# Weight parts of an FFN that begin 16-byte pieces apart inside larger buffers

## The chip, the core and the metric

The kernel runs on one core of one Trainium2 chip. The core has five engines that work side by side, each through its own queue of instructions: TensorE (PE, matrix products; its weight loads are shown apart as PEld), VectorE (DVE), ScalarE (ACT), GpSimd (POOL) and SyncE (SP, which issues the DMA transfers here). They meet in a memory of 128 rows (partitions), called SBUF; results of products land in a second one, PSUM. The metric is the device time of one execution in microseconds. Before the change it is 877.67 us, the median of three runs that lie between 876.88 and 879.24.

## The reference

One decoder layer in float32 with 512 tokens and 1024 channels. A first sub-layer has two token mixers (a sparse attention in three branches, and a gated delta rule), gates, an output projection and a layer norm. The change lies in the second sub-layer, a gated MLP with a short convolution:

```
def conv_ffn(x, w_up, conv_w, w_down):          # w_up 1024 x 5632, w_down 2816 x 1024
    h = causal_dwconv(x @ w_up, conv_w)         # width 3, along the tokens
    gate, val = jnp.split(h, 2, axis=-1)
    return (jax.nn.silu(gate) * val) @ w_down

x = layer_norm(DEEPNORM_ALPHA * x + f, ln2_g, ln2_b)   # f = conv_ffn(x, ...)
```

## The kernel before

Every large product is made of three. A float32 matrix is split in two parts, `hi`, its copy in the shortened format that TensorE takes at full pace (`F32R`), and `lo`, the rest. With both sides split, hi x hi, hi x lo and lo x hi are summed in PSUM. So each weight tile costs a copy on ACT (`wh`, line 215) and a subtraction, in the FFN on DVE (`wl`, line 219), before TensorE can use it.

`split_w` does this for one unit of weights. A unit is 512 KB: 128 partitions with 1024 values (4096 bytes) each. SP loads it into one of three `raw` buffers (line 208). Then its two halves of 512 values follow one another: the copy into one of three `wh` buffers, the subtraction into one of three `wl` buffers. Each of these holds 2048 bytes a partition, exactly one half. A buffer is written again when TensorE has done its last product with the half that it held. The buffers lie in the pool `stream`, which is used through the whole kernel, and begin at addresses that are multiples of 256 bytes; so do all the other large tiles.

The FFN runs in this order.

- **Output projection and first layer norm** (lines 953 to 975). For each of four row tiles of 128 tokens, TensorE makes two products of 512 columns (`pw`) from the parts `woh` and `wol` of the projection's weights. DVE adds the residual (line 971), takes the statistics (972) and does the norm (927 to 934, with one step on POOL, line 247). Eight transposes (line 946) turn the row tile, and ACT and DVE split it into `mh` and `ml` (948, 949). The transposes of a row tile stand in TensorE's queue inside the next tile's products; those of the last one stand behind the first two units of the FFN. This hides the norm.
- **First two channel tiles** (p = 0 and 1, lines 978 to 998). Their four units are split whole (lines 987 and 988) into buffers of their own, and their products run in two halves of 256 columns each.
- **Up projection** (lines 1006 to 1027). For each of the 20 other channel tiles, and for gate and value (b = 0, 1), one unit goes through `split_w`, and `product` (lines 229, 231, 232) makes 24 products of 512 columns into `pu`. The weight parts are the stationary side here: 128 columns of 512 bytes are loaded for each product, while `mh` or `ml` moves through. Behind them ACT, DVE and POOL do the convolution, the gate and the split into `ah` and `al`.
- **Down projection** (lines 1041 to 1066). For each half of the 1024 output channels, 11 units of two k tiles are split, and `down` (lines 1034 to 1036) makes 24 products a unit into four PSUM tiles `pdn`. The weight parts are the moving side here: rows of 512 values, 2048 bytes, stream through, and `ah` or `al` is loaded. In the second half the last four units go through other buffers (`th`, `tl`, lines 1045 to 1051), so 11 + 7 units use `split_w`. The residual and the last layer norm follow.

A planner sets each engine's order from the program's order and the times at which it believes buffers to be free; the waits come from the reads and writes of each tile's bytes.

Of the kernel before, what the change touches and what calls it, by code (L numbers as in the profile page):

```python
# [11 lines left out]
F32R = mybir.dt.float32r  # L12
# [5 lines left out]
S = 512  # L18
D = 1024
KD = 8  # L20
# [47 lines left out]
def layout(a):  # L68
# [18 lines left out]
    for i in range(8):  # L87
# [38 lines left out]
BUFS = {"in": 3, "st": 6, "mid": 4, "out": 3, "att": 4, "ob": 1, "qf": 2, "kq": 2, "lx": 1, "pg": 2, "pd": 2, "pa": 3,  # L126
        "raw": 3, "wh": 3, "wl": 3, "q2": 4, "mg": 6, "mr": 4}
# [3 lines left out]
def body(ctx: ExitStack, tc: tile.TileContext, d, out):  # L131
    nc = tc.nc
    V, A, G, PE = nc.vector, nc.scalar, nc.gpsimd, nc.tensor
# [42 lines left out]
    wp = ctx.enter_context(tc.tile_pool(name="stream", bufs=2))  # L176
# [25 lines left out]
        A.activation(xh[:, k, :], xr, AF.Copy)  # L202
        V.tensor_tensor(xl[:, k, :], xr, xh[:, k, :].bitcast(F32), op=OP.subtract)

    def split_w(src, shape, eng, first=A):

        raw = wp.tile(shape, F32, name="raw", bufs=BUFS["raw"])
        nc.sync.dma_start(out=raw, in_=src)
        half = shape[1] // 2
        hi, lo = [], []  # L210
        for i in range(2):
            r = raw[:, i * half:(i + 1) * half]
            wh = wp.tile([128, half] + list(shape[2:]), F32R, name="wh", bufs=BUFS["wh"])
            if first is A:
                A.activation(wh, r, AF.Copy)  # L215
            else:
                first.tensor_copy(wh, r)
            wl = wp.tile([128, half] + list(shape[2:]), F32R, name="wl", bufs=BUFS["wl"])
            eng.tensor_tensor(wl, r, wh.bitcast(F32), op=OP.subtract)  # L219
            hi += [wh[:, k] for k in range(half)]  # L220
            lo += [wl[:, k] for k in range(half)]
        return hi, lo

    def product(ps, w, m, n):

        (wh, wl), (mh_, ml_) = w, m
        first = None
        for k in range(n):
            i = PE.matmul(ps, wh[k], mh_(k), start=(k == 0), stop=False)  # L229
            first = first or i  # L230
            PE.matmul(ps, wh[k], ml_(k), start=False, stop=False)  # L231
            PE.matmul(ps, wl[k], mh_(k), start=False, stop=(k == n - 1))  # L232
        return first
# [3 lines left out]
    def gemm_t(u, eng=None, after=None):  # L237
        w = split_w(d["wT"][u], [128, KD, 128], E("ws", u, "G"), E("wh", u, "A"))
        ps = gps()
        first = product(ps, w, (lambda k: xh[:, k, :], lambda k: xl[:, k, :]), KD)  # L240
        if after is not None:
            tc.add_manual_dep(first.ins, after.ins.name, mybir.DependencyInfo(
                mybir.DependencyClass.NoSync, mybir.DependencyReason.SCHED_ONLY), reason="its rows have no room before")
        return ps
# [601 lines left out]
    at = 0  # L846
# [33 lines left out]
    for i in range(8):  # L880
        src = (oT + yT)[i]
# [4 lines left out]
    for m in range(8):  # L886
        while done < min(16, max(2 * m + 4, BUFS["mg"] + 2)):
            merge(done, mg2)
            done += 1
        wh, wl = split_w(d["wm"][m], [128, KD, 128], V)  # L890
        t = []
        for b in range(2):
            ps = pm.tile([128, S], F32, name=f"pm{b}")
            product(ps, (wh[4 * b:], wl[4 * b:]), (lambda k: yoh[:, 4 * b + k, :], lambda k: yol[4 * b + k]), 4)
            v = MG.pop(2 * m + b)
            V.scalar_tensor_tensor(v, v, 1.0, ps, op0=OP.add, op1=OP.mult)
            t.append(v)
        V.tensor_tensor(t[0], t[0], t[1], op=OP.add)
        A.activation(mh[:, m, :], t[0], AF.Copy)
        V.tensor_tensor(ml[:, m, :], t[0], mh[:, m, :].bitcast(F32), op=OP.subtract)  # L900
        raw = wp.tile([128, D], F32, name="raw", bufs=BUFS["raw"])
        nc.sync.dma_start(out=raw, in_=d["wo"][m])
        A.activation(woh[:, m, :], raw, AF.Copy)
        V.tensor_tensor(wol[:, m, :], raw, woh[:, m, :].bitcast(F32), op=OP.subtract)
# [19 lines left out]
    def layer_norm(r, gb, st, after=lambda i: None):  # L924

        mv = ln.tile([128, 2], F32, name="mv", bufs=2)
        V.bn_aggr(out=mv, in_=st)
        rs = ln.tile([128, 1], F32, name="rs", bufs=2)
        V.tensor_scalar(rs, mv[:, 1:2], LN_EPS, None, op0=OP.add)  # L929
        rsqrt(rs, rs, 1)  # L930
        for i in range(2):
            cs = slice(i * 512, (i + 1) * 512)
            V.scalar_tensor_tensor(r[:, cs], r[:, cs], mv[:, 0:1], gb[:, 0, cs], op0=OP.subtract, op1=OP.mult)
            V.scalar_tensor_tensor(r[:, cs], r[:, cs], rs, gb[:, 1, cs], op0=OP.mult, op1=OP.add)
            after(i)
# [44 lines left out]
    first = {}  # L980
    for p in range(NE):
        for b in range(2):
            raw = wp.tile([128, KD, 128], F32, name="raw", bufs=BUFS["raw"])
            nc.sync.dma_start(out=raw, in_=d["up"][p, :, b])
            wh = fw.tile([128, KD, 128], F32R, name=f"wh{p}{b}")
            wl = fw.tile([128, KD, 128], F32R, name=f"wl{p}{b}")
# [15 lines left out]
    ah = fp.tile([128, NF, S], F32R, name="ah")  # L1002
    al = fp.tile([128, NF, S], F32R, name="al")
    pdn = psum("pdn", 1)
    for p in range(NF):
        g = []
        for b in range(2):
            if p < NE:
                ps = first[p, b][2]
            else:  # L1010
                wu = split_w(d["up"][p, :, b], [128, KD, 128], V)
                ps = pu.tile([128, S], F32, name=f"pu{b}")
                product(ps, wu, (lambda k: mh[:, k, :], lambda k: ml[:, k, :]), KD)
            w = fcw[:, b * NF + p, :]
            acc = fs.tile([128, S], F32, name=f"fa{b}", bufs=2)
            A.activation(acc, ps, AF.Copy, scale=w[:, 2:3])  # L1016
            for i in (1, 0):
                n = 2 - i
                V.scalar_tensor_tensor(acc[:, n:], ps[:, :S - n], w[:, i:i + 1], acc[:, n:],  # L1019
                                       op0=OP.mult, op1=OP.add)  # L1020
            g.append(acc)
        th = fs.tile([128, S], F32, name="fth", bufs=1)
        A.activation(th, g[0], AF.Tanh, scale=0.5)
        V.scalar_tensor_tensor(th, th, 1.0, g[0], op0=OP.add, op1=OP.mult)
        G.tensor_tensor(th, th, g[1], op=OP.mult)  # L1025
        A.activation(ah[:, p, :], th, AF.Copy)
        V.tensor_tensor(al[:, p, :], th, ah[:, p, :].bitcast(F32), op=OP.subtract)
# [4 lines left out]
    def down(ps, k, t, wh, wl):  # L1032
        ts = slice(t * 128, (t + 1) * 128)
        PE.matmul(ps, ah[:, k, ts], wh, start=(k == 0), stop=False)  # L1034
        PE.matmul(ps, ah[:, k, ts], wl, start=False, stop=False)  # L1035
        PE.matmul(ps, al[:, k, ts], wh, start=False, stop=(k == NF - 1))  # L1036

    stats = []
    for i in range(2):
        cs = slice(i * 512, (i + 1) * 512)  # L1040
        pss = [pdn.tile([128, S], F32, name=f"pdn{t}") for t in range(TT)]
        last = []
        for k0 in range(0, NF, 2):
            if i == 1 and k0 >= NF - NL:
                raw = wp.tile([128, 2, S], F32, name="raw", bufs=BUFS["raw"])
                nc.sync.dma_start(out=raw, in_=d["down"][i, k0 // 2])
                hi = tw.tile([128, 2, S], F32R, name=f"th{k0}")
                lo = tw.tile([128, 2, S], F32R, name=f"tl{k0}")
                A.activation(hi, raw, AF.Copy)
                V.tensor_tensor(lo, raw, hi.bitcast(F32), op=OP.subtract)  # L1050
                last += [(k0 + kk, hi[:, kk], lo[:, kk]) for kk in range(2)]
                continue
            hi, lo = split_w(d["down"][i, k0 // 2], [128, 2, S], V)
            for kk in range(2):
                for t in range(TT):
                    down(pss[t], k0 + kk, t, hi[kk], lo[kk])
        for t in range(TT):
            for k, hi, lo in last:
                down(pss[t], k, t, hi, lo)
            r = x1[:, t, :]  # L1060
            V.scalar_tensor_tensor(r[:, cs], r[:, cs], ALPHA, pss[t], op0=OP.mult, op1=OP.add)
            if i == 0:
                stats.append(ln.tile([128, 2, 6], F32, name=f"st{t}"))
            V.bn_stats(out=stats[t][:, i, :], in_=r[:, cs])
            if i == 1:
                ts = slice(t * 128, (t + 1) * 128)
                layer_norm(r, ln2, stats[t], lambda j: nc.sync.dma_start(
                    out=out[ts, j * 512:(j + 1) * 512], in_=r[:, j * 512:(j + 1) * 512]))
# [22 lines left out]
```

## Time and profile before

| what | us |
|---|---|
| median of three runs | 877.67 (876.88 to 879.24) |
| the profiled execution | 879.48 |
| its span, first to last instruction | 877.7 |
| TensorE busy in the span | 847.1 (97%) |
| DVE, ACT, POOL busy | 562.6, 384.8, 159.9 |
| up projection's 960 products behind the first two channel tiles | 217.6 |

How to read it: times in a profile are counted from the start of the span. An instruction's busy time on TensorE is modelled and overlaps that of the next one, so the pace of products is read from their starts. "Idle before" is the time for which an engine stood still ahead of a group, with the instruction that ended it. The granted clock is the share of TensorE's full clock that it was given, 0.988 in the mean over the span.

### The profile page before, as it was taken

How to read it: one execution, taken by the hardware profiler on the slowest of the kernel's cores; microseconds unless marked ns; L12 is line 12 of the kernel's file. 1: busy time of each engine (PE TensorE's matmuls, PEld its weight loads, DVE VectorE, ACT ScalarE, POOL GpSimd, SP SyncE). 2: the span in 40 equal slices, each digit the busy share in tenths (PEclk: the TensorE clock that was granted, in tenths of full speed). 3: DMA queues.
4: the chain of work that ended last, by engine and by line, in shares of the span. 5: the costliest groups of instructions: out<-in, count | busy, mean ns of one | idle time of the engine just before them, and what ended most of it. 6: DMA issues, size and time to landing. Idle time of an engine off the chain costs nothing.

```text
span 877.7 us, 11725 instructions
## 1 busy us (share of the span) xinstructions
PE 847.1 (97%) x4292; PEld 698.2 (80%) x4292; DVE 562.6 (64%) x1159; ACT 384.8 (44%) x855; POOL 159.9 (18%) x141
## 2 busy tenths in 40 slices
PE   9899799999999999999999999999999999999996
PEld 8677678777777678888888898888888888888885
DVE  4755759995766987485457636777766677423337
ACT  5463268567446767443234104444444444322220
POOL 1232342324424320112100001111111111000001
PEclk9999799999999999999999999999999999999999
DMA  7323110101111001254356001333333323333322
GB/s 244 119 72 96 48 50 25 49 25 49 48 50 48 25 26 49 73 159 137 135 192 240 24 1 49 96 96 97 96 97 98 97 98 98 106 100 99 96 73 96
DMA packets 22954, 76.33 MB, mean 87 GB/s; under 512 B 3184, under 2 KB 3568, under 8 KB 22640
## 3 DMA queue, kind: packets, MB, share of 16 engines
q1 hardware_dynamic: 22896, 75.57, 26.9%
q8 instruction: 34, 0.56, 0.2%
q14 instruction: 24, 0.20, 0.1%
HBM read 73.47 MB, written 2.10 MB: 86 GB/s over the span
## 4 chain that ended last, share of the span: by engine, by line
PE 86%; DVE 9%; ACT 2%; issue 1%; DMA 1%; POOL 0%; SPq 0%; DVEq 0%; ACTq 0%; POOLq 0%
PE pu L229 9%; PE pu L231 9%; PE pu L232 9%; PE gps L229 7%; PE gps L232 7%; PE gps L231 7%; PE pdn L1036 5%; PE pdn L1034 5%; PE pdn L1035 5%; PE pout L805 2%; DVE tmp L495 2%; PE pw L969 2%; PE pw L970 2%; PE pm L232 2%; PE pm L231 2%; PE pw L968 2%
## 5 line engine op out<-in xcount | busy, mean ns | idle before, releaser
L215 ACT ACTIVATE wh<-raw 128x512 fp32r<-128x512 f32 (+1 forms) x198 | 122.6, 622 | 224.4 <-PE pu L231 99.3
L219 DVE TENSOR_TENSOR wl<-raw,wh 128x512 fp32r<-128x512 f32 (+1 forms) x172 | 134.5, 784 | 133.4 <-ACT wh L215 130.5
L229 PE MATMUL pu<-mh,wh 128*128 128x512 f32 (+1 forms) x384 | 142.7, 372 | 0.0
L231 PE MATMUL pu<-ml,wh 128*128 128x512 f32 (+1 forms) x384 | 142.6, 371 | 0.0
L232 PE MATMUL pu<-mh,wl 128*128 128x512 f32 (+1 forms) x384 | 142.6, 371 | 0.0
L229 PE MATMUL gps<-xh,wh 128*128 128x512 f32 x320 | 131.3, 411 | 0.8 <-DVE acc L372 0.5
L232 PE MATMUL gps<-xh,wl 128*128 128x512 f32 x320 | 130.4, 407 | 0.0
L231 PE MATMUL gps<-xl,wh 128*128 128x512 f32 x320 | 129.0, 403 | 0.0
L219 POOL TENSOR_TENSOR wl<-raw,wh 128x512 fp32r<-128x512 f32 x48 | 63.5, 1324 | 170.5 <-ACT wh L215 101.0
L232 PEld LDWEIGHTS pu<-mh,wl 128*128 128x128 f32 x384 | 72.3, 188 | 12.6
L229 PEld LDWEIGHTS pu<-mh,wh 128*128 128x128 f32 x384 | 72.3, 188 | 12.6
L231 PEld LDWEIGHTS pu<-ml,wh 128*128 128x128 f32 x384 | 72.3, 188 | 12.3
L1019 DVE SCALAR_TENSOR_TENSOR fa<-pu,fcw,fa 128x511 f32<-128x511 f32 x88 | 65.7, 746 | 10.7 <-ACT fa L1016 9.2
L229 PEld LDWEIGHTS gps<-xh,wh 128*128 128x128 f32 x320 | 61.3, 191 | 12.9 <-issue 1.3
L232 PEld LDWEIGHTS gps<-xh,wl 128*128 128x128 f32 x320 | 61.0, 191 | 11.2 <-POOL wl L219 0.5
L231 PEld LDWEIGHTS gps<-xl,wh 128*128 128x128 f32 x320 | 61.1, 191 | 10.6 <-issue 0.4
L1025 POOL TENSOR_TENSOR fth<-fth,fa 128x512 f32<-128x512 f32 x22 | 28.7, 1302 | 214.0 <-DVE fa L1019 214.0
L1035 PE MATMUL pdn<-wl,ah 128*128 128x512 f32 x144 | 56.0, 389 | 0.0
L1034 PE MATMUL pdn<-wh,ah 128*128 128x512 f32 x144 | 56.0, 389 | 0.0
L1036 PE MATMUL pdn<-wh,al 128*128 128x512 f32 x144 | 56.0, 389 | 0.0
L765 ACT ACTIVATE sc<-sc,mn 128x384 f32<-128x384 f32 (+2 forms) x64 | 35.7, 559 | 15.0 <-DVE mn L763 14.3
L247 POOL TENSOR_TENSOR rs<-rs,minus_half 128x1 f32<-128x1 f32 x8 | 7.5, 941 | 184.3 <-DVE rs L929 184.3
(295 smaller groups left out, 1536.8 us busy)
## 6 DMA issues: line engine op xcount, KB each, us to landing
raw<-in_up SPq DMA_DIRECT2D x44, 512.0 KB, 3.6
raw<-in_wT SPq DMA_DIRECT2D x40, 512.0 KB, 3.6
raw<-in_down SPq DMA_DIRECT2D x22, 512.0 KB, 3.4
raw<-in_wm SPq DMA_DIRECT2D x8, 512.0 KB, 3.7
raw<-in_wo SPq DMA_DIRECT2D x8, 512.0 KB, 3.5
xr<-in_xT SPq DMA_DIRECT2D x8, 256.0 KB, 4.9
ln<-in_lnr SPq DMA_DIRECT2D x2, 1024.0 KB, 5.5
xax<-in_x SPq DMA_DIRECT2D x4, 512.0 KB, 5.2
```

The source lines that it names most:

```text
L215: A.activation(wh, r, AF.Copy)
L219: eng.tensor_tensor(wl, r, wh.bitcast(F32), op=OP.subtract)
L229: i = PE.matmul(ps, wh[k], mh_(k), start=(k == 0), stop=False)
L231: PE.matmul(ps, wh[k], ml_(k), start=False, stop=False)
L232: PE.matmul(ps, wl[k], mh_(k), start=False, stop=(k == n - 1))
L495: V.tensor_tensor(tmp[:, :, :n], lx[:, :, r + 1:, r], bc(xs[:, :, r:r + 1], (128, TT, n)), op=OP.mult)
L765: A.activation(s[:, i, :n], s[:, i, :n], AF.Exp, scale=-1.0, bias=mn[:, 0, i:i + 1], accum_out=mn[:, 1, i:i + 1])
L1019: V.scalar_tensor_tensor(acc[:, n:], ps[:, :S - n], w[:, i:i + 1], acc[:, n:], op0=OP.mult, op1=OP.add)
L1025: G.tensor_tensor(th, th, g[1], op=OP.mult)
L1034: PE.matmul(ps, ah[:, k, ts], wh, start=(k == 0), stop=False)
L1035: PE.matmul(ps, ah[:, k, ts], wl, start=False, stop=False)
L1036: PE.matmul(ps, al[:, k, ts], wh, start=False, stop=(k == NF - 1))
```

## The change

In the FFN `split_w` gets a pool, `lines`, and a number `at`. The two parts of a half no longer lie in `wh` and `wl` of the pool `stream`, but in buffers `swh` and `swl` of 576 values (2304 bytes, 9 x 256), three of each, and begin `4 * at` values, that is `at` pieces of 16 bytes, into them. In the up projection `at` is p mod 16, in the down projection 4 i + k0 / 2, so it runs from 0 to 15 and from 0 to 10. The pool is opened behind `ah` and `al`; its buffers begin at multiples of 256 bytes, on space that the parts `wol` of the output projection's weights held before. The units outside the FFN, the first two channel tiles and the last four units of the down projection stay as they were.

```
-    def split_w(src, shape, eng, first=A):
+    def split_w(src, shape, eng, first=A, at=None):
...
-            wh = wp.tile([128, half] + list(shape[2:]), F32R, name="wh", bufs=BUFS["wh"])
+            part = lambda name: wp.tile([128, half] + list(shape[2:]), F32R, name=name, bufs=BUFS[name])
+            if at is not None:
+                def part(name):
+                    t = at[0].tile([128, 576], F32R, name="s" + name, bufs=BUFS[name])
+                    return t[:, 4 * at[1]:4 * at[1] + 512].rearrange("p (a b) -> p a b", a=half)
+            wh = part("wh")
...
-            wl = wp.tile([128, half] + list(shape[2:]), F32R, name="wl", bufs=BUFS["wl"])
+            wl = part("wl")
...
+    lines = ctx.enter_context(tc.tile_pool(name="lines", bufs=1, side="left"))
...
-                wu = split_w(d["up"][p, :, b], [128, KD, 128], V)
+                wu = split_w(d["up"][p, :, b], [128, KD, 128], V, at=(lines, p % 16))
...
-            hi, lo = split_w(d["down"][i, k0 // 2], [128, 2, S], V)
+            hi, lo = split_w(d["down"][i, k0 // 2], [128, 2, S], V, at=(lines, 4 * i + k0 // 2))
```

## The prediction

> **What bounds the kernel now.** I read the page's head and its chain first, then the busy time of each engine by stretch, and last the groups and the order of time inside the two stretches that the change touches.
>
> ```profile
> span 877.7 us, 11725 instructions
> PE   9899799999999999999999999999999999999996
> PE 86%; DVE 9%; ACT 2%; issue 1%; DMA 1%; POOL 0%; SPq 0%; DVEq 0%; ACTq 0%; POOLq 0%
> ```
>
> The second line is TensorE in 40 slices of 21.9 us: from the sixth slice to the last but one it is never under 90% busy. The third says that 86% of the chain that ended last is TensorE's own work. By stretch (columns: start and end, length, then busy time and instruction count of PE, PEld, DVE, ACT, POOL, then the granted clock, DMA share and GB/s):
>
> ```profile
> 462.60:508.90 46.30, 46.30 (x218) 38.49 (x217) 30.34 (x48) 13.72 (x18) 2.82 (x3) 1.00 0.35 125
> 508.90:532.80 23.90, 23.90 (x202) 23.90 (x201) 10.78 (x17) 3.68 (x6) 2.21 (x2) 1.00 0.00 1
> 532.80:750.40 217.60, 217.60 (x963) 180.16 (x961) 152.35 (x201) 97.44 (x162) 26.07 (x20) 1.00 0.30 95
> 750.40:860.90 110.50, 110.50 (x489) 91.48 (x488) 41.26 (x60) 26.59 (x40) 2.27 (x2) 1.00 0.30 95
> 860.90:877.70 16.80, 9.37 (x42) 7.42 (x40) 11.77 (x22) 0.00 (x0) 2.81 (x3) 0.90 0.25 95
> ```
>
> The first row is the output projection with the first layer norm, the second the two FFN channel tiles whose weights lie in buffers of their own, the third the other 20 channel tiles of the up projection, the fourth most of the down projection, the fifth its end and the last layer norm. The change touches the third and fourth: 960 up products and 432 down products read the moved parts. There TensorE is busy all of the time at a granted clock of 1.00, so only two things can move the end: TensorE's pace for one product, or a wait that lasts longer than its cover. The groups behind these stretches (mean ns of one after the busy time, then the idle time before them and what ended it):
>
> ```profile
> L229 PE MATMUL pu<-mh,wh 128*128 128x512 f32 x320 | 124.5, 389 | 0.0
> L1034 PE MATMUL pdn<-wh,ah 128*128 128x512 f32 x144 | 56.0, 389 | 0.0
> L1035 PE MATMUL pdn<-wl,ah 128*128 128x512 f32 x144 | 56.0, 389 | 0.0
> L229 PEld LDWEIGHTS pu<-mh,wh 128*128 128x128 f32 x384 | 72.3, 188 | 12.6
> L215 ACT ACTIVATE wh<-raw 128x512 fp32r<-128x512 f32 x113 | 71.4, 632 | 162.0 <-PE pu L231 99.3 <-PE pdn L1036 59.2 <-DVE st L1064 2.8
> L219 DVE TENSOR_TENSOR wl<-raw,wh 128x512 fp32r<-128x512 f32 x113 | 93.0, 823 | 113.5 <-ACT wh L215 113.4
> L1019 DVE SCALAR_TENSOR_TENSOR fa<-pu,fcw,fa 128x511 f32<-128x511 f32 x42 | 31.3, 744 | 1.3 <-ACT fa L1016 1.3
> L933 DVE SCALAR_TENSOR_TENSOR x<-x,mv,ln 128x512 f32<-128x512 f32 x8 | 5.6, 743 | 0.0
> ```
>
> A product's own 389 ns overlap the next one's; the pace is read from starts:
>
> ```profile
> 754.02 0.39 PE L1035 MATMUL pdn<-wl,ah 128*128 128x512 f32 x1
> 754.25 0.39 PE L1036 MATMUL pdn<-wh,al 128*128 128x512 f32 x1
> 514.39 0.28 PE L231 MATMUL pu<-ml,wh 128*128 128x256 f32 x1
> 514.51 0.28 PE L232 MATMUL pu<-mh,wl 128*128 128x256 f32 x1
> ```
>
> One product each 0.23 us with 512 columns; exactly, the third stretch holds the 960 up products (its 963 count neighbours that overlap its ends), so 217.60 / 960 = 0.2267 us. With 256 columns it is 0.12 us. The difference, 0.107 us for 256 columns, is 0.417 ns a column, and 227 - 512 x 0.417 leaves 13 ns a product that do not depend on its length.
>
> **The change, part by part.** No instruction is added or removed. In the built programs every FFN instruction behind the first channel tiles stands in the same order with the same waits. Four things differ.
>
> (1) *ACT writes and DVE reads and writes at the shifted starts.* 632 and 823 ns today. The nearest row with a shifted start is L1019, which reads and writes its sum 4 bytes past a multiple of 256: 744 ns, against 743 for L933, three operands on full multiples. So I take 0. If each split took half as long again, DVE would need 152 + 47 us of the third stretch's 218: still covered. The ring of three halves covers a late split too: ACT waits 99.3 us for TensorE to free a half, not the reverse.
>
> (2) *Weight loads of the up projection at shifted starts.* For 19 of 20 channel tiles (p mod 16 is 0 only for p = 16) the loaded 128 columns begin off a multiple of 256: 19 x 48 = 912 products. A load shows 188 ns under a pace of 227, so 39 ns more are covered even if none of the 188 is waiting. I take 0; beyond 39 ns each ns costs 0.9 us.
>
> (3) *Moving rows of the down projection at shifted starts.* Of 18 units one has the start 0, so 17 x 24 = 408 products stream 512 columns from a shifted row. No row here streams a contiguous row from a start off 256, so it is bounded. The nearest rows are two of plain float32 products, one with each column 64 bytes from the last, one contiguous:
>
> ```profile
> 69.14 4.20 PE L674 MATMUL aps<-kv,raw 128*128 128x155 f32 x15
> 66.19 1.03 PE L466 MATMUL dps<-kq 128*128 128x256 f32 x4
> ```
>
> (4.20 - 0.44) / 14 = 0.269 us for 155 columns, 1.73 ns a column; (1.03 - 0.39) / 3 = 0.213 for 256, 0.83 ns a column. A column that opens a new piece of the row costs 0.9 ns more. A shift of whole 16-byte pieces in a contiguous row opens at most one piece more: 408 x 0.9 ns = 0.4 us. Upper end: that piece is streamed in full, 16 columns (6.7 ns) if pieces are 64 bytes, 64 columns (26.7 ns) if 256: 2.7 or 10.9 us. Lower end: part of the 13 fixed ns goes, the second rival. I take 0, the row being nearest to the low end.
>
> [...]
>
> (4) *Three splits move.* The new buffers lie on the space of the output projection's weights, so the first two halves of unit (p=2, b=0) and the first of (2,1) can't be split before the last output product. In the old order they stand in the first row tile's layer norm, in the new one, in the same interleaving, in the last one's, where the transposes wait behind them:
>
> ```profile
> 474.35 0.68 DVE L971 SCALAR_TENSOR_TENSOR x<-pw,xax 128x512 f32<-128x512 f32 x1
> 476.87 0.63 DVE L219 TENSOR_TENSOR wl<-raw,wh 128x512 fp32r<-128x512 f32 x1
> 478.81 0.74 DVE L934 SCALAR_TENSOR_TENSOR x<-x,rs,ln 128x512 f32<-128x512 f32 x1
> 474.08 1.87 ACT L215 ACTIVATE wh<-raw 128x512 fp32r<-128x512 f32 x3 [0.91 <-DMA raw<-in_up]
> 509.08 0.69 DVE L971 SCALAR_TENSOR_TENSOR x<-pw,xax 128x512 f32<-128x512 f32 x1 [3.72 <-PE pw L970]
> 512.17 1.41 DVE L934 SCALAR_TENSOR_TENSOR x<-x,rs,ln 128x512 f32<-128x512 f32 x2
> 514.63 1.03 PE L946 MATMUL pt<-ident,x 128*128 128x128 f32 x8
> 515.42 0.36 PE L229 MATMUL pu<-mh,wh 128*128 128x256 f32 x1
> ```
>
> With the three subtractions inside, the chain from the projection's sum to L934 takes 478.81 - 474.35 = 4.46 us; without, 512.17 - 509.08 = 3.09. So L934 would begin at 509.08 + 4.46 = 513.54 and its two halves end at 514.28 and 514.95. TensorE reaches the transposes at 514.63; the first four need the first half (no wait), the second four would begin at about 515.03 and need the second (0.1 us to spare). The three copies on ACT (1.87 us from about 509.1) run just ahead of the subtractions. If the subtractions cost DVE their full length (0.67 each, 2.0 us in all) the second half is there at 515.6: a wait of 0.6. I take 0.1, for the thin margin, and keep 0 to 0.6. The gain in the first tile's norm is nothing: TensorE idles for 0.0 us in the first stretch. SP's two exchanged loads (a raw unit and the third row tile of x) fall before the second stretch, in which the DMA share is 0.00, and the third unit's weights are needed only at 532.8.
>
> Sum: 0 + 0 + 0 + 0.1 us. The profiled execution took 879.48 us, 1.8 above its span and above the median shown; its successor would take 879.6, and the median 877.67 becomes 877.8.
>
> **Rivals.** *A, longer moving rows (slower).* The piece that is opened beyond a row's end is streamed in full: 2.7 us (880.5) with 64-byte pieces, 10.9 us (888.7) with 256. For it: all large operands stand on multiples of 256 today, so the present 227 ns would not show it. Against: contiguous reading opens pieces far more seldom than L674. It decides from 2.6 us / 408 = 6.4 ns a product. *A2, the same for the weight loads as well:* they grow past 227 ns. 64 columns more at 188 / 128 = 1.47 ns are 94 ns, 188 + 94 = 282, 55 ns over the pace, on 912 products 50 us (with A 939); a third of that, 17 us, gives 906. Against: 256-column products run at 0.12 us with the same loads, so most of the 188 ns is waiting.
>
> *B, faster.* The fixed 13 ns a product is a collision of the load's row and the moving row, which both begin on multiples of 256, and other starts avoid it: 1320 products x 13 ns = 17 us, 861; it decides from 2 ns on. Against: the float32 rows of L466 take 0.83 ns a column, which is 2 x 0.417 with nothing left over, though in the built program they begin on such multiples too. [...]
>
> *C, the layer norm's wait.* As in (4), at its upper end 0.6 us: 878.3, within the bound.
>
> **How the numbers follow.** No change of pace, with C inside it: 0.50, its own range 876.7 to 879.5, the spread of the runs shown about 877.8. A up to 889: 0.28, of which 0.04 stays under the bound of 0.3% (2.6 us), about what a measurement of this kernel tells from no change. A2 or more: 0.12. B: 0.10, 0.01 of it too small to tell. Slower by over 0.3%: 0.24 + 0.12 = 0.36; faster 0.09; same 0.50 + 0.04 + 0.01 = 0.55. The range leaves out A2 and most of B, about 0.2: from 875.5 to 891.
>
> **What would show it.** Right: starts 0.2267 us apart in both FFN stretches at every unit's shift, 217.6 us for the 960 up products, and transposes beginning at about 514.6. Wrong: a pace that differs between units with start 0 and the others (A, only in the down projection; A2, in both; B, shorter), loads beyond 188 ns, or TensorE idle before the transposes for more than 0.6 us. The prediction fails if the read of a row depends on where in 256 bytes it begins.

## The result and the profile after

| | before | after |
|---|---|---|
| median of six runs each, us | 877.58 (876.88 to 879.24) | 885.88 (882.47 to 886.77) |
| profiled execution, us | 879.48 | 886.77 |
| its span, us | 877.7 | 884.9 |

The changed kernel takes 1.0082 times as long, with an interval of 1.0059 to 1.0105. It is slower by 0.8%. The forecast of no change, 877.8, was wrong; the time lies inside the range, 875.5 to 891, and inside rival A's 880.5 to 888.7. The page of the changed kernel (head, TensorE's share by slice, chain by engine):

```profile
span 884.9 us, 11726 instructions
PE   9899799999899899999999999999999999999996
PE 86%; DVE 9%; ACT 3%; issue 1%; DMA 0%; POOL 0%; DVEq 0%; ACTq 0%; POOLq 0%
```

Hardly anything here has changed beside the span: TensorE is still the bound and still busy everywhere in the FFN. By stretch (columns as in the prediction; the third row is one tile whose start is 8 pieces, the fourth one whose start is 12, the fifth one whose start is 0):

```profile
532.80:755.33 222.53, 222.53 (x963) 180.48 (x961) 151.17 (x201) 97.39 (x162) 26.13 (x20) 1.00 0.29 93
755.33:855.52 100.19, 100.19 (x433) 81.21 (x432) 35.45 (x49) 26.59 (x40) 1.30 (x1) 1.00 0.31 99
599.94:611.14 11.20, 11.20 (x49) 9.01 (x48) 7.53 (x10) 4.84 (x9) 1.29 (x1) 1.00 0.32 100
644.57:655.56 10.99, 10.99 (x49) 9.02 (x48) 7.60 (x10) 4.84 (x9) 1.30 (x1) 1.00 0.32 97
688.86:699.74 10.88, 10.88 (x50) 9.01 (x49) 7.61 (x10) 4.84 (x9) 1.29 (x1) 1.00 0.32 96
```

The first row is the 960 up products, 217.60 before and 222.53 now: +4.9 us. The second is the 18 units (432 products) of the down projection that the change shifts. Before, their first product began at 750.40 and the one behind them at 848.35, so 97.95 us, now 100.19: +2.2 us. Together 7.1 of the span's 7.2. The first of these stretches begins at 532.80 against 532.77 before, so next to nothing was lost ahead of it. The three single tiles have 48 products each: 233.3, 229.0 and 226.7 ns a product. With the start 0 the pace is that of before. All at a granted clock of 1.00, with TensorE busy for the whole stretch, so it is the pace of a product and not a wait or a lower clock. The groups (mean ns of one, then idle time before them and what ended it):

```profile
L235 PE MATMUL pu<-mh,swh 128*128 128x512 f32 x320 | 126.2, 394 | 0.0
L1041 PE MATMUL pdn<-swh,ah 128*128 128x512 f32 x144 | 56.7, 394 | 0.0
L1041 PE MATMUL pdn<-th,ah 128*128 128x512 f32 x32 | 12.5, 389 | 0.0
L235 PEld LDWEIGHTS pu<-mh,swh 128*128 128x128 f32 x320 | 60.2, 188 | 13.8
L225 DVE TENSOR_TENSOR swl<-raw,swh 128x512 fp32r<-128x512 f32 x113 | 91.8, 812 | 121.5 <-ACT swh L221 121.5
L221 ACT ACTIVATE swh<-raw 128x512 fp32r<-128x512 f32 x113 | 71.4, 632 | 170.1 <-PE pu L237 105.5 <-PE pdn L1043 63.8 <-DVE al L1034 0.7
```

A product with a shifted side shows 394 ns, one from the unshifted `th` 389 as before. A weight load still shows 188. ACT's copy has its 632, DVE's subtraction 812 against 823, and ACT waits for TensorE longer than before (105.5 against 99.3 us): it is the one that is ahead. The place where the three moved splits now stand:

```profile
508.98 0.69 DVE L977 SCALAR_TENSOR_TENSOR x<-pw,xax 128x512 f32<-128x512 f32 x1 [3.72 <-PE pw L976]
513.51 1.40 DVE L940 SCALAR_TENSOR_TENSOR x<-x,rs,ln 128x512 f32<-128x512 f32 x2
514.53 1.16 PE L952 MATMUL pt<-ident,x 128*128 128x128 f32 x8
515.45 0.36 PE L235 MATMUL pu<-mh,wh 128*128 128x256 f32 x1
```

From the transposes' start to the next product it is 0.92 us against 515.42 - 514.63 = 0.79 before: 0.13 us of waiting.

Mean time between product starts, worked out from the trace, by the start of the unit's parts (start of the unit's first product to that of the next unit's, divided by 24, or by 48 for the two units of an up tile):

```
start, 16-byte pieces   0     1     2     3     4     5     6     7     8     9     10    11    12    13    14    15
up (loaded), ns         226.7 226.8 233.1 233.3 233.2 231.8 234.1 233.2 233.4 233.4 233.2 229.9 229.0 233.2 233.3 227.1
down (moving), ns       226.7 231.5 233.5 233.0 229.5 230.8 233.9 230.9 232.7 233.4 233.8 -     -     -     -     -
```

The starts 2 to 5 come twice in the up projection, 4 to 10 twice in the down projection; the second time each mean is the same within 0.1 ns. So within this kernel the start sets the pace, not chance and not the place in the kernel. It is no matter of on or off 256 bytes alone: 1 and 15 cost next to nothing in the up projection (226.8 and 227.1 ns), 11 and 12 half of the rest or less (229.9 and 229.0 against 231.8 to 234.1).

### The profile page after: what moved, and what is told of

Its sections match the earlier page's. It is cut to its first block, busy times and chain, and to the rows that moved or that the text cites. A ratio compares the mean times of both kernels' runs of the same rounds, so it can differ in the third digit from the quotient of the medians.

```text
span 884.9 us, 11726 instructions
## 1 busy us (share of the span) xinstructions
PE 855.1 (97%) x4292; PEld 699.6 (79%) x4292; DVE 561.9 (64%) x1159; ACT 384.8 (43%) x855; POOL 160.1 (18%) x141
## 4 chain that ended last, share of the span: by engine, by line
PE 86%; DVE 9%; ACT 3%; issue 1%; DMA 0%; POOL 0%; DVEq 0%; ACTq 0%; POOLq 0%
PE pu L235 9%; PE pu L238 9%; PE pu L237 9%; PE gps L235 7%; PE gps L238 7%; PE gps L237 7%; PE pdn L1042 5%; PE pdn L1043 5%; PE pdn L1041 5%; PE pout L811 2%; DVE tmp L501 2%; PE pw L976 2%; PE pm L238 2%; PE pw L974 2%; PE pw L975 2%; PE pm L237 2%
## 5 line engine op out<-in xcount | busy, mean ns | idle before, releaser
L225 DVE TENSOR_TENSOR swl<-raw,swh 128x512 fp32r<-128x512 f32 x116 | 93.8, 809 | 121.5 <-ACT swh L221 121.5
L221 ACT ACTIVATE swh<-raw 128x512 fp32r<-128x512 f32 x116 | 73.1, 632 | 174.9 <-PE pu L237 105.5
L235 PE MATMUL gps<-xh,wh 128*128 128x512 f32 x320 | 131.6, 412 | 0.8 <-DVE acc L378 0.5
L238 PE MATMUL gps<-xh,wl 128*128 128x512 f32 x320 | 130.5, 408 | 0.0
L237 PE MATMUL gps<-xl,wh 128*128 128x512 f32 x320 | 129.3, 404 | 0.0
L235 PE MATMUL pu<-mh,swh 128*128 128x512 f32 x320 | 126.2, 394 | 0.0
L238 PE MATMUL pu<-mh,swl 128*128 128x512 f32 x320 | 126.0, 394 | 0.0
L237 PE MATMUL pu<-ml,swh 128*128 128x512 f32 x320 | 126.0, 394 | 0.0
L221 ACT ACTIVATE wh<-raw 128x512 fp32r<-128x512 f32 (+1 forms) x82 | 49.5, 610 | 63.5 <-PE gps L237 41.9
L235 PEld LDWEIGHTS gps<-xh,wh 128*128 128x128 f32 x320 | 61.5, 192 | 13.0 <-issue 1.3
L238 PEld LDWEIGHTS pu<-mh,swl 128*128 128x128 f32 x320 | 60.2, 188 | 14.2
L237 PEld LDWEIGHTS pu<-ml,swh 128*128 128x128 f32 x320 | 60.2, 188 | 14.0
L235 PEld LDWEIGHTS pu<-mh,swh 128*128 128x128 f32 x320 | 60.2, 188 | 13.8
L238 PEld LDWEIGHTS gps<-xh,wl 128*128 128x128 f32 x320 | 61.3, 192 | 11.2 <-POOL wl L225 0.3
L237 PEld LDWEIGHTS gps<-xl,wh 128*128 128x128 f32 x320 | 61.2, 191 | 10.7 <-issue 0.4
L225 DVE TENSOR_TENSOR wl<-raw,wh 128x512 fp32r<-128x512 f32 (+1 forms) x56 | 39.6, 711 | 21.5 <-ACT wh L221 18.7
```

## The experiments

The edits are against the changed kernel. Each time is set against runs of the kernel before on the same chip. Where no interval stands it is one execution, read by its stretches.

**Is it the start at all?** The change also moved the buffers to another place and made them longer. All starts set to 0, with the buffers where they are:

```
-                wu = split_w(d["up"][p, :, b], [128, KD, 128], V, at=(lines, p % 16))
+                wu = split_w(d["up"][p, :, b], [128, KD, 128], V, at=(lines, 0))
...
-            hi, lo = split_w(d["down"][i, k0 // 2], [128, 2, S], V, at=(lines, 4 * i + k0 // 2))
+            hi, lo = split_w(d["down"][i, k0 // 2], [128, 2, S], V, at=(lines, 0))
```

> The changed kernel with every start set to 0: same larger buffers, same place, same moved splits, but each part begins at a multiple of 256 bytes. Theory P (the pace of products depends on where rows begin): 227 ns a product in both FFN stretches, 217.6 us for the 960 up products, and the time of before, 877.6 within 1 us. Theory Q (the new place of the buffers, or the moved splits, cost it): 231 to 233 ns as with the shifts, 882 to 887 us.

Measured: median 878.27 us against 878.30, ratio 0.9996 (0.9966 to 1.0027). The two stretches of this kernel:

```profile
532.36:749.99 217.63, 217.63 (x962) 180.19 (x961) 152.42 (x201) 97.42 (x162) 26.08 (x20) 1.00 0.29 95
749.99:847.97 97.98, 97.98 (x433) 81.08 (x432) 35.48 (x49) 26.59 (x40) 1.29 (x1) 1.00 0.31 102
```

217.63 / 960 = 226.7 ns again. The new buffers, their length and the moved splits cost nothing that can be measured; all of the loss hangs on where the parts begin.

**One row's start, or how two rows stand to each other?** `mh` and `ml`, the moving side of the up projection, now also begin 4 pieces past a multiple of 256; the rest stays.

```
-    mh = mx.tile([128, KD, S], F32R, name="mh")
-    ml = mx.tile([128, KD, S], F32R, name="ml")
+    both = mx.tile([128, 2 * KD * S + 64], F32R, name="mhl")
+    mh, ml = [both[:, 16 + o:16 + o + KD * S].rearrange("p (a b) -> p a b", a=KD) for o in (0, KD * S)]
```

> The changed kernel with the moving side of the up projection (mh and ml) shifted as well, by 4 pieces (64 bytes) for all units. Theory R (what counts is how the loaded row and the moving row stand to each other within 256 bytes): the curve of the up projection moves by 4 places, 227 ns for weight shifts 3, 4 and 5 (which had 233, 233 and 232), 233 for shifts 15 and 1 (which had 227), about 229 for shift 0; the output projection, whose loaded side is now mh at shift 4 against moving rows at 0, goes from 227 to 233. Theory S (each row that begins off a multiple of 256 costs for itself, the moving and the loaded one): no up unit is at 227; shift 0 has the 229 to 230 that a moving shift of 4 has in the down projection, and the others are at 233 or more.

Measured: 884.84 us. Three tiles of this kernel by stretch, with the starts 4, 8 and 0:

```profile
553.89:564.77 10.88, 10.88 (x49) 9.01 (x48) 7.92 (x10) 4.84 (x9) 1.29 (x1) 1.00 0.33 101
598.05:609.24 11.19, 11.19 (x49) 9.02 (x48) 7.55 (x10) 4.84 (x9) 1.30 (x1) 1.00 0.32 100
687.43:698.42 10.99, 10.99 (x49) 9.02 (x48) 7.59 (x10) 4.84 (x9) 1.30 (x1) 1.00 0.32 102
```

The tile with the start 4, slow in the changed kernel, now has 10.88 / 48 = 226.7 ns. The start 0, fast there, has 229.0, which there belongs to 12, that is 0 - 4. The whole curve has moved by four places: written by the difference, loaded start minus moving start, all means agree with the row above within 0.1 ns, but for two (226.7 at 15 against 227.1, and 226.6 at 1 against 226.8, each in one of two tiles). The down projection keeps its own curve, and it is not that of the up projection written by the difference: a loaded row one piece behind the moving one has 231.5 ns there (start 1) and 227.1 here (start 15). The output projection, unshifted itself but fed from the shifted `mh`, went from 227 to 233 ns a product:

```profile
469.78 0.39 PE L974 MATMUL pw<-woh,mhl 128*128 128x512 f32 x1
470.94 0.40 PE L976 MATMUL pw<-woh,mhl 128*128 128x512 f32 x1
```

These are the first and the last of six in a row: 1.16 us for five steps. So it is neither side's start by itself. For one order of products, what counts is how the loaded row and the moving row stand to each other.

**The period, and the writes.** Starts of 16 to 55 pieces in the up projection and 11 to 28 in the down projection; and a start of 2 pieces for the last four units (`th`, `tl`), whose products run when ACT has nothing more to write.

```
-                    t = at[0].tile([128, 576], F32R, name="s" + name, bufs=BUFS[name])
+                    t = at[0].tile([128, 768], F32R, name="s" + name, bufs=BUFS[name])
...
-                wu = split_w(..., at=(lines, p % 16))
+                wu = split_w(..., at=(lines, 16 + 2 * (p - NE) + b))
...
-                hi = tw.tile([128, 2, S], F32R, name=f"th{k0}")
+                hi = tw.tile([128, 2 * S + 64], F32R, name=f"th{k0}")[:, 8:8 + 2 * S].rearrange("p (a b) -> p a b", a=2)
...
-            hi, lo = split_w(..., at=(lines, 4 * i + k0 // 2))
+            hi, lo = split_w(..., at=(lines, 11 + 11 * i + k0 // 2))
```

> The changed kernel with the 40 up units at 16 to 55 pieces (256 to 880 bytes, one more for each unit), the 18 down units at 11 to 28 pieces, and th and tl of the last four down units, which are split long before they are read, at 2 pieces. Period of 256 bytes: 227 ns at 16, 17, 31, 32, 33, 47, 48 and 49 pieces in the up projection, 233 between, and in the down projection about 231 at 15 and 17 and 227 at 16. Period of 512 bytes: 227 at 31, 32, 33 alone. No period (a cost of any start off the buffer's own): 233 throughout. Theory T (the shifted writes of ACT and DVE collide with TensorE's reads): the last four units stay at 227, because ACT and DVE have no writes left there; any theory of TensorE's own reads has them at 233.

Measured: 885.33 us. A tile of this kernel with the starts 32 and 33, one with 40 and 41, and the stretch of the last four units:

```profile
619.84:630.73 10.89, 10.89 (x50) 9.02 (x49) 7.62 (x10) 4.86 (x9) 1.30 (x1) 1.00 0.30 99
664.28:675.48 11.20, 11.20 (x49) 9.01 (x48) 7.54 (x10) 4.84 (x9) 1.29 (x1) 1.00 0.31 96
853.45:875.60 22.15, 22.15 (x96) 17.80 (x95) 13.19 (x24) 0.00 (x0) 2.87 (x3) 1.00 0.15 56
```

226.9 and 233.3 ns: 32 is as 0, 40 as 8. The curve repeats every 16 pieces, 256 bytes, in both projections, within 0.5 ns, but for the first unit of the up projection (227.8) and the start 16 of the down projection (228.3). For the down projection the run also gives the missing places (233.0 at 11, 232.9 at 12 and 14, 234.5 at 13, 227.0 at 15). The last four units ran at 233.0 to 233.3 ns with ACT at 0.00 us busy, so writes by ACT are not the cause there.

**Is it the time of the load?** In the value units, the loads for the six inner ones of the eight k tiles take 64 columns in place of 128, which leaves out half of these products' output. The starts stay.

```
-    def product(ps, w, m, n):
+    def product(ps, w, m, n, cols=128):
...
+            c = cols if 0 < k < n - 1 else 128
-            i = PE.matmul(ps, wh[k], mh_(k), start=(k == 0), stop=False)
+            i = PE.matmul(ps[:c], wh[k][:, :c], mh_(k), start=(k == 0), stop=False)
...
-                product(ps, wu, (lambda k: mh[:, k, :], lambda k: ml[:, k, :]), KD)
+                product(ps, wu, (lambda k: mh[:, k, :], lambda k: ml[:, k, :]), KD, 64 if b else 128)
```

> The changed kernel with weight loads of 64 columns in place of 128 for the six inner k of each value unit (b = 1); that part of the product is left out. Theory U (the loaded row's pieces take turns with the moving row's, so both the fixed 13 ns and the extra 6 ns come from the load): with half the load, 220 ns a product at shifts 0, 1 and 15 and 223 at the others. Theory V (a fixed start-up cost of a product, and a cost of opening the loaded row that does not depend on its length): 227 and 233 as with 128 columns. The gate units (b = 0) keep 227 and 233 in both.

Measured: 888.0 us. The loads of both lengths, and the two units of the tile with the start 0, gate with 128 columns, then value with 64:

```profile
L236 PEld LDWEIGHTS pu<-mh,swh 128*128 128x128 f32 x200 | 37.6, 188 | 9.8
L236 PEld LDWEIGHTS pu<-mh,swh 128*64 128x64 f32 x120 | 16.2, 135 | 10.6
689.99:695.43 5.44, 5.44 (x25) 4.51 (x24) 4.03 (x5) 2.46 (x5) 1.29 (x1) 1.00 0.28 88
695.43:700.93 5.50, 5.50 (x25) 3.54 (x24) 3.57 (x6) 2.36 (x5) 0.00 (x0) 1.00 0.42 115
```

Neither expectation holds. The loads are shorter by 53 ns, but the pace with the start 0 went from 226.7 to 229.2 ns, and with 1 and 15 to 231.8 and 233.5. At the starts 8 and 12 it became shorter instead (231.8 and 228.7). So a shorter load is not cheaper in itself: with 64 columns the starts have another curve.

**Starts inside a piece.** Starts in steps of one value, 4 bytes: 0 to 39 in the up projection, and in the down projection, as the edit has it, 1 to 11 in the first half and 8 to 14 in the second (not up to 18, as the expectation says).

```
-                    return t[:, 4 * at[1]:4 * at[1] + 512].rearrange("p (a b) -> p a b", a=half)
+                    return t[:, at[1]:at[1] + 512].rearrange("p (a b) -> p a b", a=half)
...
-                wu = split_w(..., at=(lines, p % 16))
+                wu = split_w(..., at=(lines, 2 * (p - NE) + b))
...
-            hi, lo = split_w(..., at=(lines, 4 * i + k0 // 2))
+            hi, lo = split_w(..., at=(lines, 1 + 11 * i + k0 // 2 - 4 * i))
```

> The changed kernel with the starts in steps of one value, 4 bytes: 0 to 39 values (0 to 156 bytes) over the 40 up units, 1 to 18 values over the 18 down units. If the rows are read in whole pieces of 16 bytes and only the piece counts, the curve is that of the pieces, drawn out four times (227 up to 4 or 7 values, then 233, with four equal units to a step), apart from starts inside a piece, which open one piece more. If the exact start counts, it changes with every value. A down unit with a start inside a piece would show the price of one piece more: 1 ns or less by the prediction's rows, 1.7 ns if a piece of 4 columns is streamed in full.

Measured: 885.25 us. There are no steps four values wide. In the up projection the starts 1, 2 and 3 have 232.3, 230.8 and 229.8 ns. Of the whole pieces, 2 to 8 agree with the changed kernel within 0.4 ns, but one piece (4 values) has 233.4 here and 226.8 there, and nine pieces (36 values) have 227.1 here and 233.4 there. So at some starts the pace also hangs on what ran before. It is not everywhere so: in the down projection 8 to 11 values come twice, and each has the same mean within 0.1 ns, though 8 values stand behind a unit of 226.7 ns the first time and behind one of 229.8 the second. Starts inside a piece can be fast, too: 30 and 39 values have 227.1 and 226.8 ns in the up projection. In the down projection 5 values give the worst pace of this kernel, 239.8, and 7 values 226.7:

```profile
776.01 0.40 PE L1042 MATMUL pdn<-swl,ah 128*128 128x512 f32 x1
777.45 0.40 PE L1042 MATMUL pdn<-swl,ah 128*128 128x512 f32 x1
...
787.82 0.39 PE L1041 MATMUL pdn<-swh,ah 128*128 128x512 f32 x1
788.50 0.39 PE L1041 MATMUL pdn<-swh,ah 128*128 128x512 f32 x1
```

The first pair is six steps apart (240 ns each), the second three (227 ns each).

**Only one part shifted.** `wl` alone in the gate units and `wh` alone in the value units, and in the down projection likewise by halves: `wl` by 4 to 14 pieces in the first, `wh` in the second by 0 to 6, as the edit has it (not 4 to 10).

```
-                    return t[:, 4 * at[1]:4 * at[1] + 512].rearrange("p (a b) -> p a b", a=half)
+                    return t[:, at[1][name]:at[1][name] + 512].rearrange("p (a b) -> p a b", a=half)
...
+ at=(lines, dict(wh=0 if b else 4 * (p % 16), wl=4 * (p % 16) if b else 0))
...
+ at=(lines, dict(wh=4 * (k0 // 2) if i else 0, wl=0 if i else 4 * (4 + k0 // 2)))
```

> The changed kernel with only one of the two weight parts shifted in the up projection: wl by p mod 16 pieces in gate units (b = 0), wh in value units (b = 1), the other part at 0. In the down projection wl is shifted by 4 to 14 pieces with wh at 0 in the first half, wh by 4 to 10 with wl at 0 in the second. If a product pays for its own pair of rows alone, a unit's mean is 227 plus a third (wl) or two thirds (wh) of what it paid with both shifted, 229 and 231 at the slow shifts, and the products that stand unshifted stay at 227. If each start depends on where the ones before it ended, all three kinds of product in a unit change together. If some mixture is faster than 227, this shows it.

Measured: 885.08 us. Most units have means of 230 to 234 ns, and no mixture goes below 226.7. Four products of a gate unit with `wl` at 4 pieces and `wh` at 0:

```profile
556.23 0.39 PE L235 MATMUL pu<-mh,swh 128*128 128x512 f32 x1
556.45 0.40 PE L237 MATMUL pu<-ml,swh 128*128 128x512 f32 x1
556.69 0.39 PE L238 MATMUL pu<-mh,swl 128*128 128x512 f32 x1
556.92 0.39 PE L235 MATMUL pu<-mh,swh 128*128 128x512 f32 x1
```

In the mean over this unit a product of L235 is followed after 226 ns, one of L237 after 236, one of L238, the only one with the shifted `wl`, after 231. L237's two rows both begin on multiples of 256, and it is the slowest. In most units all three kinds are slower than 227, in a few one kind stays at 226. A product's pace is that of its sequence, not of its own pair of rows alone.

**The changed kernel once more**, unaltered, at another time.

> The changed kernel once more, on the chip of the next one. If the pace belongs to the starts alone, each unit has the mean of its first profile within 0.5 ns, the 960 up products take 222.3 us, and the ratio to the kernel before lies near 1.008. If it comes from what else the core does at that moment, the units differ.

Measured: 885.93 us against 879.30, ratio 1.0088 (1.0059 to 1.0117). The up products:

```profile
529.81:752.34 222.53, 222.53 (x963) 180.49 (x961) 151.28 (x201) 97.43 (x162) 26.14 (x20) 1.00 0.29 93
```

It is 222.53 us to the last digit, and the units' means are the same within 0.1 ns.

**All rows alike, but off 256.** If the difference is what counts, a common start of 8 pieces for `mh`, `ml`, `ah`, `al` and all FFN parts must cost nothing. (`both` is made as above.)

```
...
+    mh, ml = [both[:, 32 + o:32 + o + KD * S].rearrange("p (a b) -> p a b", a=KD) for o in (0, KD * S)]
...
+    ah = fp.tile([128, NF * S + 64], F32R, name="ah")[:, 32:32 + NF * S].rearrange("p (a b) -> p a b", a=NF)
...
+                wu = split_w(..., at=(lines, 8))
...
+                hi = tw.tile([128, 2 * S + 64], F32R, name=f"th{k0}")[:, 32:32 + 2 * S].rearrange("p (a b) -> p a b", a=2)
...
+            hi, lo = split_w(..., at=(lines, 8))
```

> Every tile of the FFN shifted by the same 8 pieces (128 bytes): mh, ml, ah, al, the weight parts of all up and down units, th and tl. 8 pieces are among the slow shifts when only the weights have them (233.4 ns up, 232.8 ns down). If only the difference between loaded and moving row counts: 227 ns in both FFN stretches, 217.6 us for the 960 up products, while the output projection, with mh at 8 against weights at 0, goes to 233 and takes 1.2 us more: 879 us in all. If a start off 256 bytes costs for itself: 233 ns or more in both stretches, 886 us or more.

Measured: median 880.95 us against 879.30, ratio 1.0016 (0.9993 to 1.0039). Its two stretches:

```profile
530.58:748.19 217.61, 217.61 (x962) 180.24 (x961) 152.33 (x201) 97.55 (x162) 26.05 (x20) 1.00 0.30 95
748.19:846.14 97.95, 97.95 (x433) 81.09 (x432) 35.33 (x49) 26.65 (x40) 1.29 (x1) 1.00 0.32 102
```

These are the times of before, with every row of these two stretches begun in the middle of 256 bytes. So at this start being off 256 has no price of its own (226.7 ns a product in both stretches); only standing unlike has (233.4 and 232.7 ns with the weights alone at 8 pieces). The weights of the first two channel tiles and of the output projection stay at 0. The output projection took 47.0 us from its first product's start to its last's, against 46.1: 0.9 us more, where 1.2 were expected.

**All rows alike inside a piece.** As the last, with 5 values (20 bytes) for each of these starts in place of 32.

> As the run before with all FFN tiles alike, but at 5 values (20 bytes), a start inside a 16-byte piece, where a row of 512 values touches one piece more; weights alone at 5 values had 232.7 ns up and 239.8 ns down. If only the difference of the two starts counts, and one piece more costs nothing: 227 ns in both stretches, 217.6 us for the 960 up products. If one piece more costs what the prediction bounded (0.9 to 6.7 ns a product): 228 to 234 ns, the same for all units.

Measured: 901.45 us against 878.81. The two stretches:

```profile
541.28:767.82 226.54, 226.54 (x962) 181.66 (x961) 150.13 (x201) 97.38 (x162) 26.16 (x20) 1.00 0.28 91
767.82:869.34 101.52, 101.52 (x433) 81.69 (x432) 35.42 (x49) 26.71 (x40) 1.29 (x1) 1.00 0.29 98
```

236.0 and 235.0 ns a product in the mean: 8 to 9 more, though the rows stand alike. Nor is it the same for all units: in the up projection every fourth has 239.5 ns and the others 234.6 to 235.5, all with the same starts. So being alike is not enough. It cost nothing at 0, 4 and 8 whole pieces (226.7 ns) and cost this at 5 values, the only start inside a piece that was tried on both sides; that every start inside a piece has a price is not shown (7 values with the weights alone had 226.7 ns). Some 7 us more of this run lie ahead of the output projection, in work that the edit does not touch (its granted clock from 100 to 200 us is 0.88 against 0.95 before).

## Why the prediction was right or wrong, step by step

The forecast was no change, and the kernel lost 0.8%. That the time still lies in the stated range is luck: the range was kept wide for rival A, and A's mechanism is not what the runs show.

- **What bounds the kernel**: right. The end moved by what TensorE's pace moved, 7.1 of 7.2 us; the only wait found is one of 0.13 us, see (4).
- **(1) ACT and DVE at shifted starts, 0**: right. 632 and 812 ns, and ACT waits for TensorE for longer than before.
- **(2) Weight loads of the up projection, 0**: this step failed, and with the larger sum. It argued that a load shows 188 ns under a pace of 227 and so has 39 ns of cover. The load did not grow by one ns, and the pace still did: 4.9 us on 912 products, 5.4 ns each. The overlap was no proof: the loaded row's start changed the pace while the load stayed under its cover.
- **(3) Moving rows of the down projection, 0**: failed as well. 2.2 us on 408 products is 5.5 ns each, between the bounds of 0.9 and 6.7, and nothing like the row that it was held nearest to. The bounds were built on the moving row alone. The run with all rows alike at 8 pieces shows that this picture is wrong even where its size is near: there a shifted row costs nothing (97.95 us, as before), as the other is shifted alike. That a column pays 0.9 ns for a piece that it opens was the author's reading of two float32 rows (1.73 and 0.83 ns a column); no run shows such a piece or its size.
- **(4) The moved splits, 0.1 us**: right. L940 (L934 before) began at 513.51 where 513.54 was forecast, and 0.13 us were lost.
- **Rival A** had the sign and a range that holds the time, by another mechanism. It placed all of the loss in the down projection, where 2.2 us alone would have stayed under the bound of 0.3%. **A2** had the loss in both projections, as it came, but needed loads beyond 188 ns; there were none. **B** named the right pair, the loaded and the moving row, and the right suspicion that both begin on multiples of 256; but their standing alike at 0, 4 or 8 pieces, with 226.7 ns, is the best case found, not a collision. With 512 columns no start tried went below 226.6 ns, so none avoids the 13 ns that the prediction worked out as fixed.
- The sentence at the end, that the prediction fails if the read of a row depends on where in 256 bytes it begins, was near: the pace depends on where two rows begin against each other, and on the products before.

What stays open: what in the memory or in TensorE has the period of 256 bytes, why the starts within a slow unit follow short cycles (such as 232, 226, 229 ns at 12 pieces), why a load of half the length has another curve, why one and nine pieces have two paces and equal starts at 5 values every fourth unit slower, and what the fixed 13 ns are. The writes of ACT are excluded for the last four units (233 ns with ACT at 0.00 us busy); reads and writes by DVE and the DMA transfers were not taken away one by one, but in the changed kernel the means came back within 0.1 ns at every repetition of a start, which speaks against both without excluding them. None of the versions beat the kernel before.

## What to carry to other kernels

The present pace of a stream of products that each load their weights can rest on an accident of layout: here that the loaded and the moving row begin at the same place within 256 bytes (226.7 ns a product, 233.4 with the weights alone 8 pieces further). When a buffer is padded, packed or sliced, keep the starts of stationary and moving operands alike modulo 256 bytes, at a start that was measured. Alike at 0, 64 (in the up projection alone) and 128 bytes cost nothing here, 226.7 ns; alike at 20 bytes took 235 to 236. Unlike starts were sometimes as fast (226.7 ns at 7 values in the down projection) and mostly 1 to 3% slower a product (229 to 234 ns). And a cover worked out from durations, here 39 ns beside a load of 188, did not show that a shifted load is free: the load stayed at 188 ns, and the pace grew by 5.4 ns a product. The pace of starts, unit by unit, shows it.

## What the runs showed beside that

- The price is exactly repeatable: 222.53 us for 960 products in both profiles of the changed kernel, where the whole time spreads over 4 us. The spread comes from elsewhere: the first product of the output projection began at 459.6 and 462.6 us in these two runs of the same kernel, with a granted clock of 0.97 and 0.95 from 100 to 200 us.
- A start can have two paces: one piece 226.8 and 233.4 ns, nine pieces 233.4 and 227.1, in kernels that differ in the units before. So a measurement of one start needs the sequence of the real kernel around it.
- With 256 columns the sign differed: with `mh` and `ml` 4 pieces further, the products of the first two channel tiles, whose weights stay at 0, came every 118 ns against 120. On their 192 products that is 0.4 us, too little to measure.
